# Fetching an expert's two rows with one gather, and working on them a step apart

## The chip, the cores and the metric

The kernel runs on one core of a Trainium2 chip. Its time is the device time of one execution in microseconds (us). The engines are TensorE (PE, with its weight loads PEld), VectorE (DVE), ScalarE (ACT), GpSimd (POOL) and SyncE (SP); each works through its own queue in order, and queues wait for each other by semaphores. DMAs are issued from SP, ACT and POOL; the indirect ones (gathers by a column of row numbers) from POOL.

## The reference, cut to what matters

Two transformer-like blocks over 512 tokens of 1024 features, fp32. The change is in the expert layer of the first block: each token has 8 heads x 16 chosen experts, 128 (expert, gate) pairs out of 16384 experts with a row of `expert_u` and a row of `expert_v` each.

```python
def block(args):                       # 128 tokens
    xb, ib, gb = args
    ug = expert_u[ib]
    act = jax.nn.gelu(jnp.einsum("td,tkd->tk", xb, ug)) * gb
    vg = expert_v[ib]
    return jnp.einsum("tk,tkd->td", act, vg)
```

## The kernel before

`run` (L1980) calls the stages in order: `mix`, `peer`, a tail and a gate (`ple`), `ssm`, `ffn`, `attn`, `ffn`. The kernel orders its instructions by hand: code that is called first stands first in the queues of its engines. Work beside the matmuls is kept in a list `self.bg` of (cost, function) pairs, and `run_bg` (L200) takes from it at a rate per matmul unit; `later` and `tick` (L92, L97) put a function off by some units.

In `peer` (L624) the 512 tokens are treated in two ways. Tokens 128 to 511 go through a dense sweep over all experts: for each of 128 groups of 128 experts (a unit `e` of `dense`, L1002) PE multiplies a strip of `exp_u` with the normed tokens (`lin`, tile `mm`, only for groups not worked out ahead), ACT takes the Gelu, DVE multiplies with the gates `G` (tile `ga`, L1039) and splits it into a high and a low part `A` (L117 on ACT, L112 on DVE), and PE multiplies `A` with a strip of `exp_v` into six accumulators `pv` (L1077). Strips come by SP (`wr`, L135); each is split into `wh` on ACT (L148) and `wl` on DVE (L150). 56 of the 128 units have their `exp_u` part done ahead, in the stage in which the gates are made.

The first 128 tokens do without the sweep. `first_block` (L961) has, for each of the 128 pairs, a gather of one row per token (128 tokens x 1024 floats, 512 KB; L974): first the rows of `expert_u`, whose dot with the token DVE forms (L987, accumulated into a column of `s`), and, after a Gelu over all 128 columns (L991) and a product with the gates (L992), the rows of `expert_v`, which DVE adds up with the activation as a scalar (L998). The first 32 (`EARLY`) dots run while the gates are made and use quarters of the tile `x`, whose content waits in DRAM (`xd`); it is loaded back in unit 16 of the sweep (L1069). The other 96 dots and 128 sums are steps of cost 1.2 in the sweep's list, with six slots of the tile `gx` and gathers five steps ahead:

```python
            a, b, k = (0, E, 3) if i < E else (E, 2 * P, 5)
            ...
            if i + k < b:
                fetch(i + k)
```

Between these steps the list has the items of `ssm_prep` (L1158): at first small DVE operations, then 16 parts of POOL operations (`bbs` with the tiles `bu`, `bv`, `bb`, `bd`, `cn`, L1320 to L1331; `wc`, `w2`, `tn`, L1339 to L1395), a few small matmuls (`m1p`, `m2p`, L1367, L1358), copies from PSUM (`m1o`, `m2o`) and stores from ACT's queue (L1361, L1383, L1401, L1402). Behind the sweep `peer_tail` (L745) turns the sums and adds them to `x` (L761).

Of the kernel before, what the change touches and what calls it, by code (L numbers as in the profile page):

```python
# [8 lines left out]
F32 = mybir.dt.float32  # L9
F32R = mybir.dt.float32r  # L10
BF16 = mybir.dt.bfloat16
I32 = mybir.dt.int32
U16 = mybir.dt.uint16
AF = mybir.ActivationFunctionType
ALU = mybir.AluOpType
# [4 lines left out]
P = 128  # L20
# [16 lines left out]
class K:  # L37
# [586 lines left out]
    def peer(self):  # L624
        nc, I = self.nc, self.I
# [3 lines left out]
        gd = self.dp.tile([NC, P, P, TC], F32, name="gd")  # L629
        sd = self.dp.tile([R, P, TD], F32, name="sd")  # L630
        xd = self.dp.tile([P, KT, T], F32, name="xd")
        so = self.tc.tile_pool(name="po", bufs=1)
        self.first = so.__enter__().tile([P, 4, P], F32, name="first")
        st = self.tc.tile_pool(name="pk", bufs=1)
        self.st = self.pk = st.__enter__()
        iota = self.loc((P, P), tag="iota")
        nc.scalar.dma_start(iota, I["c_iota"])

        iotaP = self.bank("mmc", (P, P), "held")
# [14 lines left out]
        n = self.ap.tile([P, KT, 2, TD], F32R, tag="xn", name="n", bufs=2)  # L654
        nt = self.accs.rearrange("p a b -> p (a b)")
# [55 lines left out]
        for what, i in self.q_order()[2:]:  # L711
# [5 lines left out]
            if (what, i) == ("q", 11):  # L717
                self.run_bg(1000)
                part = self.plan_choice(vals, idx, iotaP, st_["rc"])
# [4 lines left out]
        sg = self.tc.tile_pool(name="pg", bufs=1)  # L724
        self.st = sg.__enter__()

        if self.EARLY:
            nc.scalar.dma_start(xd, self.x)
        step = self.first_block(nt)
        self.plan_gates(part, iota, iotaP, gd, step)  # L730
        self.bg_rate, self.credit = sum(c for c, _ in self.bg) / (R - done - self.RB), 0
        for e in range(done, R):
            self.lin(nr, p_s(e), w=TD)
# [143 lines left out]
    def plan_gates(self, part, iota, iotaP, gd, step):  # L877
# [80 lines left out]
        bg += [(0.0, lambda: mid(n - 1)), (0.0, lambda: back(n - 2)), (0.0, lambda: back(n - 1)), (0.0, rest)]  # L958
        self.bg += bg

    def first_block(self, nt):  # L961

        nc, I = self.nc, self.I
        gate, ei, s, act = (self.first[:, j, :] for j in range(4))
        ei = ei.bitcast(I32)
        rows = [I["rows_u"], I["exp_v"].rearrange("a b d -> (a b) d")]
        x = self.x.rearrange("p (a b) t -> p a (b t)", b=2)
        E = self.EARLY

        def slot(i):  # L970
            return x[:, i % 4, :] if i < E else self.gx[:, i % 6, :]

        def fetch(i):
            nc.gpsimd.indirect_dma_start(  # L974
                out=slot(i), out_offset=None, in_=rows[i // P], in_offset=bass.IndirectOffsetOnAxis(ap=ei[:, i % P : i % P + 1], axis=0)
            )

        def step(i):
            a, b, k = (0, E, 3) if i < E else (E, 2 * P, 5)
            if i == a:  # L980
                for j in range(a, a + k):
                    fetch(j)
            if i + k < b:
                fetch(i + k)
            g, j = slot(i), i % P
            if i < P:
                nc.vector.scalar_tensor_tensor(  # L987
                    out=g, in0=g, scalar=1.0, in1=nt, op0=ALU.mult, op1=ALU.mult, accum_out=s[:, j : j + 1]
                )
                if j == P - 1:  # L990
                    nc.scalar.activation(act, s, AF.Gelu_apprx_tanh)  # L991
                    nc.vector.tensor_tensor(act, act, gate, ALU.mult)  # L992
                return
            acc = self.gx[:, 7, :]
            if j == 0:
                nc.vector.tensor_scalar(out=acc, in0=g, scalar1=act[:, j : j + 1], scalar2=None, op0=ALU.mult)
            else:
                nc.vector.scalar_tensor_tensor(out=acc, in0=g, scalar=act[:, j : j + 1], in1=acc, op0=ALU.mult, op1=ALU.add)  # L998

        return step  # L1000

    def dense(self, nr, gd, sd, xd, step):  # L1002

        nc = self.nc
        TC, R, TD, GG = self.TC, self.R, self.TD, self.GG
        NC = TD // TC
        A, G, S = {}, {}, {}
        pv = [self.px_(name="pv") for _ in range(4)]
        pv += [self.bank(tag, name="pv") for tag in ("mmb", "mmc")]
        self.mm_tags, self.few = ("mma",), True  # L1010
        gx = self.gx = self.ap.tile([P, 8, 8 * P], F32, tag="xn", name="gx", bufs=2)
        items = [(1.2, lambda i=i: step(i)) for i in range(self.EARLY, 2 * P)]
        prep = self.ssm_prep()
        np_ = len(prep)
        self.bg = []
        for i, it in enumerate(items):
            self.bg += prep[np_ * i // len(items) : np_ * (i + 1) // len(items)] + [it]
        total = sum(c for c, _ in self.bg)
        slow = self.SLOW
        L = self.LEAD  # L1020
        ahead = {e: i for i, e in enumerate(self.ahead())}
        rates = [1.0 if e + L in ahead or e + L >= P else slow for e in range(P)]
        scale = total / sum(rates[:-2])
        rates = [r * scale for r in rates]

        def load(e):
            if e >= P:
                return
            if e % GG == 0:
                t = self.loc((P, NC, GG, TC), tag="G", bufs=2)  # L1030
                nc.sync.dma_start(t, gd[:, :, e : e + GG, :].rearrange("c p e t -> p c e t"))
                G[e // GG] = t
            if e in ahead:
                S[e] = self.tmp((P, TD), tag="gs")
                nc.sync.dma_start(S[e], sd[ahead[e]])

        def gated(e, s):
            t = self.tmp((P, TD), tag="ga")
            nc.vector.tensor_tensor(  # L1039
                t.rearrange("p (c t) -> p c t", t=TC), s.rearrange("p (c t) -> p c t", t=TC), G[e // GG][:, :, e % GG, :], ALU.mult  # L1040
            )
            a = self.loc((P, 2, TD), F32R, tag="A", bufs=self.LEAD + 1)
            self.split(a[:, 0, :], a[:, 1, :], t, lag=int(e > 1))
            A[e] = a

        def p_s(e):
            def f(ps):
                s = self.tmp((P, TD), tag="gs")
                nc.scalar.activation(s, ps, AF.Gelu_apprx_tanh)
                gated(e, s)  # L1050
            return f

        def unit_u(e):
            load(e + 4)
            if e in ahead:
                self.prep_to(self.at + 1 + self.LA)
                gated(e, S.pop(e))
            elif e < P:
                self.lin(nr, p_s(e), w=TD)

        self.bg_rate = 0
        for e in range(4):
            load(e)
        for e in range(L):
            unit_u(e)
        for e in range(P):
            unit_u(e + L)
            if e == 16 and self.EARLY:
                nc.scalar.dma_start(self.x, xd)  # L1069
            s, a = self.next_strip(), A.pop(e)  # L1070
            for b in range(3):
                o = slice(b * P, b * P + P)
                for i, (x, ws) in enumerate(((0, (s.hi, s.lo)), (1, (s.hi,)))):
                    for w in ws:
                        for h in range(2):
                            last = e == P - 1 and x == 1
                            nc.tensor.matmul(pv[2 * b + h], a[:, x, o], w[:, h * T : h * T + T], start=(e == 0 and i == 0 and w is s.hi), stop=last)  # L1077
            self.tick()
            self.run_bg(rates[e])
            if e == P - 2:  # L1080
                self.ple_fetch(0)
        self.run_bg(100000)
        self.drain()
        for b in range(3):
            nc.scalar.copy(gx[:, b, 0:T], pv[2 * b])
            nc.vector.tensor_copy(gx[:, b, T:], pv[2 * b + 1])
        self.mm_tags, self.few = self.ALL, False
        return gx
# [992 lines left out]
def host(inputs):  # L2081
    import numpy as np

    i = {k: np.asarray(v) for k, v in inputs.items()}
    A = {"vecs": pack_vecs(i), "c_ident": np.eye(P, dtype=np.float32)}
# [4 lines left out]
    A["w_q"] = strips(i["w_q"][0])  # L2090
    A["skT"] = np.ascontiguousarray(i["sub_keys"][0].reshape(16, P, P).transpose(2, 0, 1))
    A["exp_u"] = np.ascontiguousarray(i["expert_u"][0].reshape(P, P, KT, P).transpose(0, 3, 2, 1).reshape(P, P, KT * P))
    A["rows_u"] = np.ascontiguousarray(i["expert_u"][0])
    A["exp_v"] = np.ascontiguousarray(i["expert_v"][0].reshape(P, P, KT * P))
    for j, (p, pe, pg) in enumerate([(i["p"][0], i["w_pe"][0], i["w_pg"][0])] + [(i["p_2"][l], i["ple_w_proj_2"][l], i["ple_w_gate_2"][l]) for l in (0, 1)]):
        A[f"pT{j}"] = fm(p[0])
# [46 lines left out]
```

## Time and profile before

| | us |
|---|---|
| median of the runs (lowest, highest) | 3119.45 (3111.47, 3125.9) |
| profiled execution | 3122.41 |
| its span, first to last instruction | 3120.6 |
| PE busy in the span | 2923.9 |
| DVE busy | 2216.9 |
| ACT busy | 1266.7 |
| POOL busy | 1183.6 |

The page's span holds all stages; the change is in those of 390 to 1720 us, and most of it in the sweep, 760 to 1690 us. A share over the whole span says little of that stretch, so the views below are cut to it. A matmul's record is longer than the time until the next one starts, since matmuls are pipelined. In a group's row the last part is the engine's idle time just before such instructions, and which instruction or DMA ended it.

### The profile page before, as it was taken

What the parts mean: (1) busy time and instruction counts of PE and PEld (TensorE: products, weight loads), DVE (VectorE), ACT (ScalarE), POOL (GpSimd) and SP (SyncE); (2) the same over time, 40 slices, a digit from 0 to 9 for tenths busy, and PEclk for the clock granted to TensorE, in tenths of its full rate; (3) what the DMA queues carried; (4) which work ended last, traced back from release to release, by engine and by line L of the source; (5) the groups of instructions that cost most, each with busy time, mean ns of one, the idle gap of its engine ahead of it and who ended that gap; (6) DMA issues with size and microseconds to landing.
All of it is one profiled execution on the core that took longest, in us unless ns stands there. A gap on an engine that the chain in (4) does not pass through costs nothing. (4 is left out here: it accounts for less than half of the span.)

```text
span 3120.6 us, 39487 instructions
## 1 busy us (share of the span) xinstructions
PE 2923.9 (94%) x14359; PEld 2456.2 (79%) x14359; DVE 2216.9 (71%) x3786; ACT 1266.7 (41%) x2016; POOL 1183.6 (38%) x1032
## 2 busy tenths in 40 slices
PE   8999988888999999999998989999999998999998
PEld 6677888787888787878877768888877766888886
DVE  7946888995898878787887684565675457566665
ACT  4333256566433333333334533433344345433333
POOL 3224565653248879788886330000011011100001
PEclk9889999999999999999999989999999989999999
DMA  4124344778788888888986283233332211233322
GB/s 138 48 84 150 105 142 163 248 252 305 252 290 304 291 314 299 307 286 305 317 291 221 89 256 103 86 101 98 97 97 88 81 40 49 93 97 101 95 73 96
DMA packets 248891, 534.77 MB, mean 171 GB/s; under 512 B 36671, under 2 KB 129219, under 8 KB 248314
## 3 DMA queue, kind: packets, MB, share of 16 engines
q1 hardware_dynamic: 170570, 343.69, 33.7%
q0 software_dynamic: 38656, 140.74, 13.0%
q10 hardware_dynamic: 39472, 47.84, 4.4%
q8 instruction: 113, 1.85, 0.2%
q14 instruction: 80, 0.66, 0.1%
HBM read 468.75 MB, written 63.44 MB: 171 GB/s over the span
## 5 line engine op out<-in xcount | busy, mean ns | idle before, releaser
L150 DVE TENSOR_TENSOR wl<-wr,wh 128x1024 fp32r<-128x1024 f32 (+2 forms) x453 | 548.7, 1221 | 456.4 <-ACT wh L148 447.6
L148 ACT ACTIVATE wh<-wr 128x1024 fp32r<-128x1024 f32 (+2 forms) x552 | 545.7, 997 | 505.5 <-PE mm L163 209.9
L161 PE MATMUL mm<-xn,wh 128*128 128x512 f32 x1296 | 521.4, 402 | 12.9 <-ACT xn L119 7.6
L163 PE MATMUL mm<-xn,wh 128*128 128x512 f32 x1296 | 512.4, 395 | 5.8 <-DVE xn L114 5.8
L162 PE MATMUL mm<-xn,wl 128*128 128x512 f32 x1296 | 512.8, 396 | 2.0 <-POOL wl L150 1.9
L230 POOL TENSOR_TENSOR accs<-accs,sq 128x512 f32<-128x512 f32 x56 | 86.2, 1540 | 1014.1 <-ACT sq L229 1009.2
L1077 PE MATMUL pv<-wh,A 128*128 128x512 f32 x1536 | 443.2, 402 | 22.5 <-DVE A L112 10.1
L150 POOL TENSOR_TENSOR wl<-wr,wh 128x1024 fp32r<-128x1024 f32 x99 | 241.1, 2436 | 450.4 <-ACT wh L148 439.4
L1077 PEld LDWEIGHTS pv<-wh,A 128*128 128x128 f32 x1536 | 291.8, 193 | 89.0 <-DVE A L112 17.6
L162 PE MATMUL mm<-n,wl 128*128 128x384 f32 x1024 | 348.3, 340 | 13.5 <-DVE wl L150 11.7
L161 PE MATMUL mm<-n,wh 128*128 128x384 f32 x1024 | 352.7, 344 | 0.8 <-ACT gs L703 0.8
L163 PE MATMUL mm<-n,wh 128*128 128x384 f32 x1024 | 347.8, 340 | 3.1 <-DVE n L114 3.1
L161 PEld LDWEIGHTS mm<-xn,wh 128*128 128x128 f32 x1296 | 248.6, 192 | 68.4 <-ACT xn L119 8.1
L163 PEld LDWEIGHTS mm<-xn,wh 128*128 128x128 f32 x1296 | 248.0, 191 | 61.4 <-DVE xn L114 8.6
L162 PEld LDWEIGHTS mm<-xn,wl 128*128 128x128 f32 x1296 | 248.6, 192 | 55.9 <-POOL wl L150 2.3
L1077 PE MATMUL pv<-wl,A 128*128 128x512 f32 x768 | 245.3, 401 | 26.6 <-DVE wl L150 26.6
L117 ACT ACTIVATE A<-ga 128x384 fp32r<-128x384 f32 x128 | 67.3, 525 | 424.6 <-DVE ga L1039 421.4
L998 DVE SCALAR_TENSOR_TENSOR gx<-gx,first 128x1024 f32<-128x1024 f32 x127 | 178.9, 1409 | 59.6 <-DMA gx<-in_exp_v,first 57.9
L162 PEld LDWEIGHTS mm<-n,wl 128*128 128x128 f32 x1024 | 196.0, 191 | 17.8 <-DVE wl L150 13.9
L161 PEld LDWEIGHTS mm<-n,wh 128*128 128x128 f32 x1024 | 196.0, 191 | 5.2 <-issue 1.6
L1077 PEld LDWEIGHTS pv<-wl,A 128*128 128x128 f32 x768 | 145.9, 192 | 67.4 <-DVE wl L150 35.1
L163 PEld LDWEIGHTS mm<-n,wh 128*128 128x128 f32 x1024 | 195.9, 191 | 3.5 <-DVE n L114 3.5
(409 smaller groups left out, 5356.4 us busy)
## 6 DMA issues: line engine op xcount, KB each, us to landing
wr<-in_exp_u SPq DMA_DIRECT2D x128, 512.0 KB
wr<-in_exp_v SPq DMA_DIRECT2D x128, 512.0 KB
wr<-in_w_up SPq DMA_DIRECT2D x88, 512.0 KB
gd<-gb ACTq DMA_DIRECT2D x48, 512.0 KB
G<-gd SPq DMA_DIRECT2D x32, 768.0 KB
wr<-in_w_dn SPq DMA_DIRECT2D x64, 320.0 KB
wr<-in_w_pg SPq DMA_DIRECT2D x24, 512.0 KB
sd<-gs SPq DMA_DIRECT2D x56, 192.0 KB
```

The source lines that it names most:

```text
L117: nc.scalar.activation(hi, src, AF.Copy)
L148: nc.scalar.activation(s.hi, s.raw, AF.Copy)
L150: eng.tensor_tensor(s.lo, s.raw, s.hi.bitcast(F32), ALU.subtract)
L161: t.matmul(ps, wh, xh, start=start, stop=False)
L162: t.matmul(ps, wl, xh, start=False, stop=False)
L163: t.matmul(ps, wh, xl, start=False, stop=stop)
L230: self.later(1, lambda: nc.gpsimd.tensor_tensor(acc, acc, sq, ALU.add))
L998: nc.vector.scalar_tensor_tensor(out=acc, in0=g, scalar=act[:, j : j + 1], in1=acc, op0=ALU.mult, op1=ALU.add)
L1077: nc.tensor.matmul(pv[2 * b + h], a[:, x, o], w[:, h * T : h * T + T], start=(e == 0 and i == 0 and w is s.hi), stop=last)
```

## The change

The host lays `expert_u` and `expert_v` side by side (`rows_uv`, a row of 2048 floats per expert). For the first 32 pairs the early dots fetch the first half of a row and the sweep the second, by the row numbers 2e and 2e + 1 in a new tile `two`. For the other 96 pairs one gather fetches both halves (1 MB). There are five slots of two rows: two in `x`, three in `gx`. A step `j` of the sweep adds pair `j - 2`, fetches pair `j + 3`, takes Gelu and gate of pair `j - 1` on ACT (two activations of one column each), and forms the dot of pair `j`. Steps with a dot cost 2.4 in the list. Since `x` now holds slots, it is loaded back in unit 125, and the rates are such that the list is done by then.

```diff
-        rows = [I["rows_u"], I["exp_v"].rearrange("a b d -> (a b) d")]
+        rows = I["rows_uv"]
+        half = rows.rearrange("e (h d) -> (e h) d", h=2)
+        pairs = self.x.rearrange("p (a b) t -> p a (b t)", b=4)
+        E, k = self.EARLY, self.SLOTS - 2
...
+        def early(i):
+            if i == 0:
+                nc.vector.tensor_scalar(out=self.two[:, 0, 0:E], in0=ei[:, 0:E], scalar1=1, scalar2=None, op0=ALU.logical_shift_left)
+                nc.vector.tensor_scalar(out=self.two[:, 1, 0:E], in0=self.two[:, 0, 0:E], scalar1=1, scalar2=None, op0=ALU.bitwise_or)
...
+        def slot(j):
+            j %= self.SLOTS
+            return pairs[:, j, :] if j < 2 else self.gx[:, 2 * j - 4 : 2 * j - 2, :].rearrange("p a b -> p (a b)")
+        def fetch(j):
+            if j < E:
+                gather(slot(j)[:, 8 * P :], half, self.two[:, 1, j : j + 1])
+            else:
+                gather(slot(j), rows, ei[:, j : j + 1])
+        def gated(a, b):
+            nc.scalar.activation(act[:, a:b], s[:, a:b], AF.Gelu_apprx_tanh)
...
+        def step(j):
+            if j == 0:
+                for i in range(k):
+                    fetch(i)
+                if E:
+                    gated(0, E)
+                    nc.vector.tensor_tensor(act[:, 0:E], act[:, 0:E], gate[:, 0:E], ALU.mult)
+            if j > 1:
+                add(j - 2)
+            if j + k < P:
+                fetch(j + k)
+            if E < j <= P:
+                gated(j - 1, j)
+                nc.scalar.activation(act[:, j - 1 : j], act[:, j - 1 : j], AF.Copy, scale=gate[:, j - 1 : j])
+            if E <= j < P:
+                dot(j, slot(j)[:, 0 : 8 * P])
...
-        items = [(1.2, lambda i=i: step(i)) for i in range(self.EARLY, 2 * P)]
+        items = [(1.2 if j < E or j >= P else 2.4, lambda j=j: step(j)) for j in range(P + 2)]
...
-        scale = total / sum(rates[:-2])
+        scale = total / sum(rates[:-4])
...
-            if e == 16 and self.EARLY:
-                nc.scalar.dma_start(self.x, xd)
...
+            if e == P - 3:
+                self.run_bg(100000)
+                nc.scalar.dma_start(self.x, xd)
```

Line numbers of the changed kernel are those of its own file: the dot is L980, the gather L977, the Gelu L1004, the sum L1011, the scaled copy L1027, the product `ga` L1076, `bbs` L1358 to L1369.

POOL's queue in the middle of the sweep, around one `bbs` (`bu` to `cn`), before:

```order
L974 DMA gx<-in_exp_v,first 128x1024 x3
L1320 TENSOR_TENSOR bu_10686<-bc_10376,s_1119_6471 128x32
L1321 TENSOR_TENSOR bv_10687<-bc_10376,s_1119_6471 128x32
L1322 TENSOR_TENSOR bb_10685<-bu_10686,bv_10687 128x32
L1323 TENSOR_TENSOR bu_10686<-bc_10376,s_1119_6471 128x32
L1324 TENSOR_TENSOR bv_10687<-bc_10376,s_1119_6471 128x32
L1325 TENSOR_TENSOR bb_10685<-bu_10686,bv_10687 128x32
L1327 MEMSET bd_10694 128x128
L1328 COPY bd_10694<-bb_10685 64x4x16
L1329 COPY bd_10694<-bb_10685 64x4x16
L1331 TENSOR_SCALAR cn_10698<-bc_10376 128x64
L974 DMA gx<-in_exp_v,first 128x1024 x5
```

And with the change, around a corresponding one:

```order
L977 DMA x<-in_rows_uv,first 128x2048
L1358 TENSOR_TENSOR bu_10179<-bc_9931,s_1119_6474 128x32
L1359 TENSOR_TENSOR bv_10180<-bc_9931,s_1119_6474 128x32
L1360 TENSOR_TENSOR bb_10178<-bu_10179,bv_10180 128x32
L1361 TENSOR_TENSOR bu_10179<-bc_9931,s_1119_6474 128x32
L1362 TENSOR_TENSOR bv_10180<-bc_9931,s_1119_6474 128x32
L1363 TENSOR_TENSOR bb_10178<-bu_10179,bv_10180 128x32
L1365 MEMSET bd_10187 128x128
L1366 COPY bd_10187<-bb_10178 64x4x16
L1367 COPY bd_10187<-bb_10178 64x4x16
L1369 TENSOR_SCALAR cn_10191<-bc_9931 128x64
L977 DMA gx<-in_rows_uv,first 128x2048 x3
```

Eight gathers of 1024 columns around a block have become four of 2048. The second copy into `bd` (L1329, now L1367) waits for all gathers in flight in both. From the first `bbs` to the end POOL's queue has 195 gathers before and 102 now; in the whole program 256 and 160.

DVE's queue over one unit of the sweep (two strips, their `ga`, then the steps), before:

```order
L112 TENSOR_TENSOR A_11714<-ga_11712,A_11714 128x384
L998 SCALAR_TENSOR_TENSOR gx<-gx,first 128x1024 x2
L150 TENSOR_TENSOR wl_11748<-wr_11666,wh_11747 128x1024
L150 TENSOR_TENSOR wl_11779<-wr_11716,wh_11778 128x1024
L1039 TENSOR_TENSOR ga_11804<-gs_11802,G_11385 128x384
L998 SCALAR_TENSOR_TENSOR gx<-gx,first 128x1024 x2
```

And with the change:

```order
L112 TENSOR_TENSOR A_12249<-ga_12247,A_12249 128x384
L1011 SCALAR_TENSOR_TENSOR gx<-gx,first 128x1024
L980 SCALAR_TENSOR_TENSOR x,first<-x,accs 128x1024
L150 TENSOR_TENSOR wl_12294<-wr_12191,wh_12293 128x1024
L150 TENSOR_TENSOR wl_12325<-wr_12251,wh_12324 128x1024
L1076 TENSOR_TENSOR ga_12350<-gs_12348,G_11960 128x384
L1011 SCALAR_TENSOR_TENSOR gx<-x,first,gx 128x1024
L980 SCALAR_TENSOR_TENSOR gx,first<-gx,accs 128x1024
```

Two sums per unit have become one sum and one dot, at the same place behind `ga`.

ACT's queue with the change, around the stores of one prep part (L1439, L1440; `first` holds the activations):

```order
L1004 ACTIVATE first<-first 128x1
L1027 ACTIVATE first<-first 128x1
L148 ACTIVATE wh_10655<-wr_10568 128x1024
L117 ACTIVATE A_10661<-ga_10659 128x384
L1439 DMA m3d<-wc_1777_10348 64x2x128 x2
L1439 DMA m3d<-wc_1790_10421 64x2x128 x2
L1440 DMA csd<-tn_10505 128x256
L1004 ACTIVATE first<-first 128x1
L1027 ACTIVATE first<-first 128x1
L148 ACTIVATE wh_10697<-wr_10599 128x1024
```

The rows of one column (L1004, L1027) are new, once per unit; the others stand as they did.

## Rows read from the trace of the kernel before

**Rows 1.** view by stretches, us: each engine's busy time, granted clock, DMA share, GB/s.

```profile
950.00:1690.00 740.00, 692.88 (x3303) 593.40 (x3302) 595.27 (x606) 240.75 (x340) 622.94 (x611) 0.97 0.87 300
```

**Rows 2.** groups on POOL, 950 to 1690 us: busy us, mean ns | idle before, releasers.

```profile
L974 POOL DMA_INDIRECT gx<-in_exp_v,first x128 | 169.5, 1325 | 32.3 <-issue 22.7 <-DVE A L112 2.4 <-DVE gx L998 2.2
L974 POOL DMA_INDIRECT gx<-in_rows_u,first x60 | 81.2, 1354 | 14.3 <-issue 9.6 <-DVE A L112 1.2 <-DVE gx L987 0.9
...
L1329 POOL COPY bd<-bb 64x64 f32<-64x64 f32 x15 | 10.5, 699 | 54.7 <-DMA gx<-in_exp_v,first 33.0 <-DMA gx<-in_rows_u,first 21.6
```

**Rows 3.** timeline of POOL, 1297 to 1318 us: start, us, instruction [idle before].

```profile
1299.25 1.32 POOL L974 DMA_INDIRECT gx<-in_exp_v,first  x1 [0.30 <-issue]
...
1309.55 0.23 POOL L1329 COPY bd<-bb 64x64 f32<-64x64 f32 x1 [5.79 <-DMA gx<-in_exp_v,first]
...
1310.41 1.02 POOL L974 DMA_INDIRECT gx<-in_exp_v,first  x1 [0.16 <-issue]
```

**Rows 4.** who waited for whom, 950 to 1690 us: us, times, longest.

```profile
ACT A L117 <- DVE ga L1039: 355.2, 98, 13.1
DVE gx L998 <- DMA gx<-in_exp_v,first: 56.7, 19, 6.8
DVE gx L987 <- DMA gx<-in_rows_u,first: 44.7, 18, 5.1
...
DVE wl L150 <- ACT wh L148: 28.0, 25, 6.3
...
ACT wh L148 <- DMA wr<-in_exp_v: 26.0, 9, 9.2
```

**Rows 5.** timeline of PE, 1303.8 to 1312.5 us.

```profile
1304.28 0.33 PE L161 MATMUL mm<-n,wh 128*128 128x384 f32 x1
...
1308.44 0.62 PE L1077 MATMUL pv<-wh,A 128*128 128x512 f32 x2
...
1311.65 0.62 PE L1077 MATMUL pv<-wl,A 128*128 128x512 f32 x2
```

**Rows 6.** groups on PE, 950 to 1690 us (L161 and L163 are x440 too).

```profile
L1077 PE MATMUL pv<-wh,A 128*128 128x512 f32 x1199 | 345.8, 401 | 8.7 <-DVE A L112 6.0 <-ACT wh L148 2.6
L1077 PE MATMUL pv<-wl,A 128*128 128x512 f32 x600 | 191.8, 401 | 26.6 <-DVE wl L150 26.6
...
L162 PE MATMUL mm<-n,wl 128*128 128x384 f32 x440 | 150.4, 342 | 11.9 <-DVE wl L150 11.7
...
L1367 PE MATMUL m1p<-wc,bd 128*32 128x128 f32 x120 | 15.9, 276 | 0.0
L1358 PE MATMUL m2p<-ident,w 128*128 128x128 f32 x64 | 9.6, 272 | 0.0
```

**Rows 7.** group on DVE, 950 to 1690 us: the product over 128 columns.

```profile
L992 DVE TENSOR_TENSOR first<-first 128x128 f32<-128x128 f32 x1 | 0.3, 292 | 0.4 <-ACT first L991 0.4
```

**Rows 8.** groups on ACT: the Gelu over 128 columns, and a table load.

```profile
L991 ACT ACTIVATE first<-first 128x128 f32<-128x128 f32 x1 | 0.3, 311 | 4.1 <-DVE gx L987 4.1
...
L1049 ACT ACT_TABLE_LOAD x1 | 1.3, 1283 | 0.0
```

**Rows 9.** view by stretches: the ten us of the reload of x.

```profile
873.00:883.00 10.00, 10.00 (x52) 9.05 (x51) 8.97 (x27) 3.95 (x6) 1.25 (x2) 1.00 1.02 415
```

**Rows 10.** timelines of ACT, PE and DVE at the end of the sweep.

```profile
1687.91 0.53 ACT L117 ACTIVATE A<-ga 128x384 fp32r<-128x384 f32 x1 [2.88 <-DVE ga L1039]
...
1695.52 1.18 PE L1077 MATMUL pv<-wh,A 128*128 128x512 f32 x4 [3.85 <-DVE A L112]
...
1702.73 0.68 DVE L761 TENSOR_TENSOR x<-x,pt 128x512 f32<-128x512 f32 x1
```

**Rows 11.** the page, part 3, DMA queues: packets, MB, share of 16 engines.

```profile
q1 hardware_dynamic: 170570, 343.69, 33.7%
q0 software_dynamic: 38656, 140.74, 13.0%
```

**Rows 12.** timeline of ACT, 1303 to 1313 us: behind prep's stores.

```profile
1311.56 2.00 ACT L148 ACTIVATE wh<-wr 128x1024 fp32r<-128x1024 f32 x2 [6.83 <-DMA m3d<-wc]
```

More of the change, by code (lines that the diff above doesn't have):

```diff
@@ L632, in peer @@
         so = self.tc.tile_pool(name="po", bufs=1)
-        self.first = so.__enter__().tile([P, 4, P], F32, name="first")
+        po = so.__enter__()
+        self.first = po.tile([P, 4, P], F32, name="first")
+        self.two = po.tile([P, 2, self.EARLY], I32, name="two")
         st = self.tc.tile_pool(name="pk", bufs=1)
@@ L725, in peer @@
         self.st = sg.__enter__()
[L727 to L730, printed above, removed]
+        nc.scalar.dma_start(xd, self.x)
+        early, step = self.first_block(nt)
+        self.plan_gates(part, iota, iotaP, gd, early)
         self.bg_rate, self.credit = sum(c for c, _ in self.bg) / (R - done - self.RB), 0
@@ L959, in plan_gates @@
         self.bg += bg
+    SLOTS = 5
     def first_block(self, nt):
@@ L965, in first_block @@
         ei = ei.bitcast(I32)
-        rows = [I["rows_u"], I["exp_v"].rearrange("a b d -> (a b) d")]
+        rows = I["rows_uv"]
+        half = rows.rearrange("e (h d) -> (e h) d", h=2)
         x = self.x.rearrange("p (a b) t -> p a (b t)", b=2)
[L968 to L994, printed above, removed]
+        pairs = self.x.rearrange("p (a b) t -> p a (b t)", b=4)
@@ new lines, in first_block, with gather, dot @@
+        E, k = self.EARLY, self.SLOTS - 2
+        def gather(dst, src, j):
+            nc.gpsimd.indirect_dma_start(out=dst, out_offset=None, in_=src, in_offset=bass.IndirectOffsetOnAxis(ap=j, axis=0))
+        def dot(j, u):
+            nc.vector.scalar_tensor_tensor(out=u, in0=u, scalar=1.0, in1=nt, op0=ALU.mult, op1=ALU.mult, accum_out=s[:, j : j + 1])
+        def early(i):
+            if i == 0:
+                nc.vector.tensor_scalar(out=self.two[:, 0, 0:E], in0=ei[:, 0:E], scalar1=1, scalar2=None, op0=ALU.logical_shift_left)
+                nc.vector.tensor_scalar(out=self.two[:, 1, 0:E], in0=self.two[:, 0, 0:E], scalar1=1, scalar2=None, op0=ALU.bitwise_or)
+            for j in range(3) if i == 0 else ():
+                gather(x[:, j % 4, :], half, self.two[:, 0, j : j + 1])
+            if i + 3 < E:
+                gather(x[:, (i + 3) % 4, :], half, self.two[:, 0, i + 3 : i + 4])
+            dot(i, x[:, i % 4, :])
@@ new lines, in slot, with add @@
+        def slot(j):
[8 more added lines that the diff above has]
+            nc.scalar.activation(act[:, a:b], s[:, a:b], AF.Gelu_apprx_tanh)
+        def add(j):
+            v, a, acc = slot(j)[:, 8 * P :], act[:, j : j + 1], self.gx[:, 7, :]
@@ L995, in step @@
             if j == 0:
-                nc.vector.tensor_scalar(out=acc, in0=g, scalar1=act[:, j : j + 1], scalar2=None, op0=ALU.mult)
+                nc.vector.tensor_scalar(out=acc, in0=v, scalar1=a, scalar2=None, op0=ALU.mult)
             else:
-                nc.vector.scalar_tensor_tensor(out=acc, in0=g, scalar=act[:, j : j + 1], in1=acc, op0=ALU.mult, op1=ALU.add)
-        return step
+                nc.vector.scalar_tensor_tensor(out=acc, in0=v, scalar=a, in1=acc, op0=ALU.mult, op1=ALU.add)
@@ L1002, in dense @@
+        return early, step
     def dense(self, nr, gd, sd, xd, step):
@@ L1011, in dense @@
         gx = self.gx = self.ap.tile([P, 8, 8 * P], F32, tag="xn", name="gx", bufs=2)
-        items = [(1.2, lambda i=i: step(i)) for i in range(self.EARLY, 2 * P)]
+        E = self.EARLY
+        items = [(1.2 if j < E or j >= P else 2.4, lambda j=j: step(j)) for j in range(P + 2)]
         prep = self.ssm_prep()
@@ L1015, in dense @@
         self.bg = []
-        for i, it in enumerate(items):
-            self.bg += prep[np_ * i // len(items) : np_ * (i + 1) // len(items)] + [it]
+        costs, at, to = sum(c for c, _ in items), 0.0, 0
+        for it in items:
+            at += it[0]
+            n = round(np_ * at / costs)
+            self.bg += prep[to:n] + [it]
+            to = n
         total = sum(c for c, _ in self.bg)
@@ L2092, in host @@
     A["exp_u"] = np.ascontiguousarray(i["expert_u"][0].reshape(P, P, KT, P).transpose(0, 3, 2, 1).reshape(P, P, KT * P))
-    A["rows_u"] = np.ascontiguousarray(i["expert_u"][0])
+    A["rows_uv"] = np.concatenate([i["expert_u"][0], i["expert_v"][0]], axis=1)
     A["exp_v"] = np.ascontiguousarray(i["expert_v"][0].reshape(P, P, KT * P))
```

## The prediction

> **What bounds the kernel now.** I read first the view by stretches: 760 to 1690 us is the dense sweep, with the gathers in it, and from 950 us on the operations of `ssm_prep` that run on GpSimd stand between the gathers. In these 740 us POOL is busy 622.9 and TensorE (PE) 692.9 us [rows 1]. The groups on POOL [rows 2] account for the rest of its time: 188 gathers, 250.7 us busy (169.5 + 81.2) and 46.6 us idle before them (32.3 + 14.3, mostly "issue", in which it waited for nothing shown), and 54.7 us idle before the copy `bd` of L1329. 622.9 + 46.6 + 54.7 = 724.2 of 740: POOL hardly ever waits for another engine's compute. **It is the saturated engine there.** Its timeline [rows 3] shows a block: a gather at 1299.25, then the operations of `bbs`, in which the copy waits 5.79 us for the gathers in flight to land; only at 1310.41 do gathers go on.
>
> Who pays stands in the waits [rows 4]: VectorE (DVE) waits 56.7 + 44.7 = 101.4 us for gathers, in 37 pieces. DVE's whole idle time is 740 - 595.3 = 144.7 us [rows 1], so gathers are 70% of it. Behind those sums in DVE's queue stand the low parts `wl` for which PE waits (26.6 and 11.7 us), and `A` (6.0 us) [rows 6].
>
> How much can PE give back? Its busy time is no floor, because matmuls overlap; the cadence is. 24 of the 384-wide follow each other from 1304.28 to 1308.44, 0.1733 us each, and 14 of the 512-wide from 1308.44 to 1311.65, 0.2293 us each [rows 5]. The stretch has 1199 + 600 wide and 3 x 440 narrow ones [rows 6]: 1799 x 0.2293 + 1320 x 0.1733 = 641 us, and 25 us of small ones (15.9 + 9.6): 666 us. **The room is 740 - 666 = 74 us.** The granted clock of 0.97 [rows 1], between the two levels of 1.2 and 2.4 GHz, says that 3% of 740 = 22 us of it is lost to stretches at the lower one; the rest is standing still.
>
> The Trainium skill ("Trainium Kernel Development and Optimization", Performance Expectations) says that matmul busy time is a bad metric and that the busy share of LDWEIGHTS is a good one. By the latter, 593.4 of 740 us, the room would be 147 us; by the former, 47 us. The cadence rows lie between the two, and I go by them.
>
> **The change part by part.**
>
> *Gathers on POOL.* The 195 gathers behind the first `bbs` become 102 (counted in the order of POOL's instructions): 93 go. One costs 250.7 / 188 = 1.33 us and 46.6 / 188 = 0.25 us of idle, 1.58 us in all [rows 2]. No row shows one of 8 KB a token. Bounds: 1.02 us, as a cheap one of 4 KB took [rows 3], and twice the mean, 2.67 us. I take 1.33, since both lists have 128 rows and the instruction is otherwise the same. POOL gets back 93 x 1.58 = 147 us; at the upper bound 147 - 102 x 1.33 = 11 us.
>
> *The copy that waits for all gathers in flight* stays, with up to four of 1 MB under way in place of five of 512 KB. Its 15 waits cost 54.7 us, 3.6 us each [rows 2]. Bounds: nothing (the gathers are spaced wider) and 110 us (each waits twice as long). I take 75 us, 20 more. POOL is left with 740 - 147 + 20 = 613 us, below PE's 666: POOL no longer sets the pace; PE does, with DVE's stalls on top.
>
> *What PE gets back.* 70% of 74 us is 52 us. A gather behind each block will still be late at times, since the lead stays about three sweep units (five steps at some 1.8 a unit before, three at one a unit now). I leave one fifth: **-42 us**. The bounds are 0 and -74.
>
> *DVE.* Dots and sums keep number and shape: 0. The product over 128 columns, 0.29 us [rows 7], shrinks to 32; two integer operations over 32 columns come before the first early dot, and by the same row cost +0.6 us at most; I take +0.4.
>
> *ScalarE (ACT).* 96 x 2 activations over one column are new; the nearest row is 0.31 us over 128 columns [rows 8]: 60 us at most, on an engine that is busy 240.8 of 740 us [rows 1]. A Gelu waits for the dot of the step before. That dot stands in DVE's queue ahead of the `ga` product for which ACT waits 355.2 us anyway [rows 4], so nothing new is waited for. The sum two steps behind needs the scaled value; ahead of it DVE has at least one `wl` whose `wh` stands later in ACT's queue. Both are hidden: 0; if that cover fails, see the slower rival. One more table load falls between Exp and Sin at the start: +1.3 us [rows 8].
>
> *The reload of `x`* moves from unit 16 to unit 125. Where it is it costs PE nothing (10.00 busy of 10 us [rows 9]). At the end it is issued behind ACT's last `A`; before, that `A` stands at 1687.91, and `x` is first added to at 1702.73 [rows 10]: 14.8 us, 11 without the stall of 3.85 us between them. 2.1 MB take 5.1 us at 415 GB/s [rows 9] and 7.0 at the stretch's 300 [rows 1]. It fits: 0, at worst +5.
>
> *The tail.* PE stands 3.85 us before the last units [rows 10], behind prep's last stores in ACT's queue. Now prep and gathers end before unit 125: -3 us.
>
> *DMA bytes* are the same. Queue q0, with the gathers, takes 13.0% for 140.74 MB, q1 33.7% for 343.69 MB of mostly shorter packets [rows 11]: 1.08 and 1.02 MB per thousandth. Longer packets gain nothing by their length: 0.
>
> **Sum.** The profiled execution took 3122.4 us (span 3120.6); the median of the runs, 3119.45, is 3 us lower, which I leave aside. 3122.4 - 42 - 3 + 0.4 + 1.3 = **3079 us**.
>
> **Rivals.**
>
> *More:* with POOL free, all 74 us go: 3122.4 - 74 - 3 + 1.7 = 3047. For it: POOL's list comes out 53 us below PE's. Against: DVE's 28.0 us of waits for `wh` [rows 4], which are not the gathers'. Chance 0.10.
>
> *POOL stays saturated,* because a row of 8 KB costs twice as much (11 us back, 20 more in the copy): 3110 to 3122. For it: the trace has gathers of one size only. Chance 0.13.
>
> *The gathers crowd out the strips.* ACT waits 26.0 us for strips of `exp_v`, in 9 pieces [rows 4]. If packets twice as long add one and a half times that, 39 us, and it passes through `wh` and `wl` to PE, the gain is gone: 3079 + 39 = 3118. Against: 10 us at 415 GB/s went by with PE fully busy [rows 9], so the engines have room. The Trainium skill ("DMA: Bandwidth & Descriptors", Queues, rings and completion order) says that an engine goes round its queues packet by packet. By that rule longer packets take a larger share from the strips; no row shows both lengths side by side. Chance 0.06.
>
> *Slower: ACT holds the sums.* The two small activations stand behind prep's stores, for which ACT's next activation waited 6.83 us [rows 12]. If DVE's sum waits for them, with some 2.5 us of `m1o` and `m2o` ahead, each of 15 parts costs DVE 9.4 us: 141 us, against the 101.4 for gathers that it saves. That is +40: 3162. It decides from 101.4 / 15 = 6.8 us a part on. Against: the `wl` ahead of the sum. Chance 0.10.
>
> *The change relieves POOL, but PE's stalls hang on ACT's stores,* and DVE's waits only move from the gather to `wh`: 40% of the gain, 3122 - 17 = 3105. Chance 0.06.
>
> **How the numbers follow.** The forecast has the rest, 0.55, and reaches from 3062 to 3098 with its terms' bounds. A measurement of this kernel can tell 0.5%, 15.6 us, from no change: below 3104 is faster. Faster: 0.55 + 0.10 + 0.05 of the cases near 3104 = 0.70. Same: 0.20. Slower: 0.10. The range runs from the larger gain to the unchanged cases, 3047 to 3122; outside lie the slower rival and a little on either side.
>
> **What would show it.** Right: POOL's busy time in the sweep falls by 100 us or more, DVE's waits for gathers fall below 40 us, the sweep from the first `bbs` on is some 40 us shorter, and its granted clock rises above 0.97. A gather of 2048 columns near 1.3 us shows the first step right, near 2.7 wrong. The forecast is wrong if DVE's sums (L1011) wait for ACT L1027, if the copy of `bd` waits over 100 us, or if the first addition to `x` waits for its reload.

## The result, and the profile after

The changed kernel takes **3078.1 us** (median; 3077.74 to 3078.62), the kernel before, run beside it, 3122.2: a ratio of 0.986, with a 95% interval of 0.9839 to 0.988. A later set of runs gave 0.9827 (0.9802 to 0.9852). The forecast was 3079. The page's busy times over the whole span:

```profile
PE 2908.9 (95%) x14359; PEld 2445.6 (79%) x14359; DVE 2218.9 (72%) x3788; ACT 1303.4 (42%) x2209; POOL 1093.8 (36%) x936
```

PE does the same matmuls; POOL has lost 90 us, ACT gained 37.

Where it was gained stands in the view by stretches, in columns as [rows 1], here from 950 to 1640 us, as far as both kernels are in the sweep; before:

```profile
950.00:1640.00 690.00, 644.49 (x3065) 551.75 (x3064) 553.86 (x569) 223.40 (x316) 580.27 (x571) 0.97 0.87 302
```

and with the change:

```profile
950.00:1640.00 690.00, 668.83 (x3248) 573.87 (x3247) 599.46 (x638) 275.23 (x529) 524.70 (x507) 0.99 0.89 321
```

In the same 690 us PE did 3248 matmuls in place of 3065, at a granted clock of 0.99 in place of 0.97, and POOL was busy 525 us in place of 580. The sweep ends earlier. The timeline around its end:

```profile
1653.40 0.62 PE L1112 MATMUL pv<-wh,A 128*128 128x512 f32 x2
...
1657.15 1.28 DVE L762 TENSOR_TENSOR x<-x,pt 128x512 f32<-128x512 f32 x2
```

The first addition to `x`, at 1702.73 us before [rows 10], begins at 1657.15, 45.6 us earlier; the span (now 3076.5) is 44.1 shorter. So all of the gain is in the sweep. The groups on POOL, 950 to 1640 us, which answer to [rows 2]:

```profile
L977 POOL DMA_INDIRECT gx<-in_rows_uv,first x55 | 78.2, 1421 | 46.2 <-DVE gx L1011 37.2 <-issue 6.6 <-DVE x L980 0.3
L977 POOL DMA_INDIRECT x<-in_rows_uv,first x38 | 52.4, 1378 | 28.9 <-DVE gx L1011 17.0 <-DVE gx L980 6.3 <-issue 4.1
...
L1367 POOL COPY bd<-bb 64x64 f32<-64x64 f32 x15 | 7.6, 504 | 40.2 <-DMA x<-in_rows_uv,first 17.7 <-DMA gx<-in_rows_uv,first 16.4 <-issue 6.0
```

A gather of 128 x 2048 costs POOL 130.6 / 93 = 1.40 us, hardly more than the 1.33 of one of 128 x 1024 [rows 2]. And POOL now waits for DVE (37.2 + 17.0 + 6.3 us), that is, for a slot to come free: the gatherer is ahead of the user. The waits of the same stretch say it from the other side:

```profile
ACT A L117 <- DVE ga L1076: 285.9, 99, 7.1
DVE wl L150 <- ACT wh L148: 87.8, 46, 7.4
...
ACT first L1004 <- DMA m3d<-wc: 47.1, 9, 7.7
```

DVE's 101.4 us of waits for gathers [rows 4] are gone: no such row is left (one of 7.4 us stands ahead of the stretch). In their place stands DVE's wait for `wh`, 87.8 us, three times what it was (28.0).

### The profile page after: what moved, and what is told of

Same layout as the page of the kernel before. It is cut to its first block, busy times and chain, and to the rows that moved or that the text cites. A ratio compares the mean times of both kernels' runs of the same rounds, so it can differ in the third digit from the quotient of the medians.

```text
span 3076.5 us, 39413 instructions
## 1 busy us (share of the span) xinstructions
PE 2908.9 (95%) x14359; PEld 2445.6 (79%) x14359; DVE 2218.9 (72%) x3788; ACT 1303.4 (42%) x2209; POOL 1093.8 (36%) x936
## 5 line engine op out<-in xcount | busy, mean ns | idle before, releaser
L161 PE MATMUL mm<-xn,wh 128*128 128x512 f32 x1296 | 520.9, 402 | 14.3 <-ACT xn L119 8.9
L163 PE MATMUL mm<-xn,wh 128*128 128x512 f32 x1296 | 512.4, 395 | 5.8 <-DVE xn L114 5.8
L161 PE MATMUL mm<-n,wh 128*128 128x384 f32 x1024 | 350.6, 342 | 0.8 <-ACT gs L705 0.8
L163 PE MATMUL mm<-n,wh 128*128 128x384 f32 x1024 | 345.9, 338 | 3.1 <-DVE n L114 3.1
L161 PEld LDWEIGHTS mm<-xn,wh 128*128 128x128 f32 x1296 | 248.5, 192 | 69.3 <-ACT xn L119 8.9
L163 PEld LDWEIGHTS mm<-xn,wh 128*128 128x128 f32 x1296 | 247.7, 191 | 61.4 <-DVE xn L114 8.3
L161 PEld LDWEIGHTS mm<-n,wh 128*128 128x128 f32 x1024 | 194.5, 190 | 4.9 <-issue 1.4
L163 PEld LDWEIGHTS mm<-n,wh 128*128 128x128 f32 x1024 | 194.0, 189 | 3.4 <-DVE n L114 3.4
L1670 ACT ACTIVATE uc<-up,vec 128x512 f32<-128x512 f32 x88 | 71.8, 816 | 203.8 <-DVE up L1668 203.8
```

Source lines behind the costliest of these rows:

```text
L161: t.matmul(ps, wh, xh, start=start, stop=False)
L163: t.matmul(ps, wh, xl, start=False, stop=stop)
L1670: nc.scalar.activation(c, u, AF.Identity, scale=w(2), bias=cb[:, m : m + 1])
```

## The experiments

Four sets of runs, each beside the kernel before on its chip (3122 to 3129 us from set to set), so ratios are compared and not microseconds. The theory is the prediction's: the number of gathers among `ssm_prep`'s operations on POOL was the price. The first rival is that it was the new order: a longer lead, both rows of an expert mixed, sums two steps behind. Windows below are 950 to 1640 us where no other is given.

| kernel | ratio to before (95%) | DVE waits for gathers, us | mean `wl` on DVE, ns |
|---|---|---|---|
| before | 1 | 95.0 | 1403 |
| changed | 0.986 (0.9839 to 0.988) | 0 | 1380 |
| e9_after, the same again | 0.9827 (0.9802 to 0.9852) | 0 | 1382 |
| e1_split | 0.9981 (0.9965 to 0.9997) | 74.5 | 1377 |
| e2_lean (of before) | 0.9777 (0.9754 to 0.98) | 0 | 1331 |
| e3_dummy | 0.9951 (0.9932 to 0.997) | 9.6 | 1480 |
| e4_tail (of before) | 1.0023 (1.0006 to 1.004) | 100.7 | 1415 |
| e5_fill | 0.9872 (0.9848 to 0.9897) | 12.6 | 1381 |
| e6_nodelay | 0.9964 (0.995 to 0.9977) | 0 | 1400 |
| e7_sp | 0.9794 (0.9774 to 0.9814) | 0.3 | 1348 |
| e8_leanfill (of before) | 0.9852 (0.9831 to 0.9873) | 56.7 | 1332 |
| e10_before_sp | 0.9967 (0.9951 to 0.9984) | 122.6 | 1426 |
| e11_sp_all | 0.9851 (0.9831 to 0.9872) | 0 | 1342 |
| e12_fill2 | 1.0061 (1.004 to 1.0083) | 115.9 | 1375 |

**e9_after: the yardstick of the last set.**

> The changed kernel once more, beside the others of this set, as what they are measured against: 0.984 to 0.988 of the kernel before.

3078.5 us, 0.9827, just below the expected range; DVE's waits and operations as in the table. The same kernel thus gave 0.986 and 0.9827 in two sets: differences of 0.3% between sets are not told apart.

**e1_split: the count of gathers alone, undone.**

```diff
-                gather(slot(j), rows, ei[:, j : j + 1])
+                gather(slot(j)[:, 0 : 8 * P], half, both[:, j : j + 1])
+                gather(slot(j)[:, 8 * P :], half, both[:, P + j : P + j + 1])
```

(`both` holds 2e and 2e + 1, written once into the free eighth of `gx`.)

> The changed kernel, but each of the 96 pairs is fetched by two gathers of 1024 columns into the two halves of the same slot; order, lead, slots and sums as changed. Theory (POOL's time in the sweep is what was bought): 96 more gathers at 1.4 + 0.25 us put some 150 us back on POOL, which had about 85 us to spare; POOL waits for nothing again, DVE waits for gathers 60 us or more, and the time is 3100 to 3122. Rival (the new order, lead or mixing of the two rows is what helps): 3078 within 8.

3119.6 us: 0.9981. Of POOL's groups and the waits:

```profile
L977 POOL DMA_INDIRECT gx<-in_rows_uv,gx x110 | 140.0, 1272 | 27.8 <-issue 18.9 <-DVE wl L150 3.0 <-DVE A L112 2.4
L977 POOL DMA_INDIRECT x<-in_rows_uv,gx x73 | 98.5, 1349 | 18.0 <-issue 12.3 <-DVE wl L150 1.8 <-DVE gx L980 0.9
```

```profile
DVE gx L980 <- DMA gx<-in_rows_uv,gx: 55.4, 18, 6.7
...
DVE x L980 <- DMA x<-in_rows_uv,gx: 19.1, 8, 4.8
```

POOL waits mostly for "issue" again, DVE waits 74.5 us for gathers, and nearly the whole gain is gone. Beside a saturated POOL, order, lead, delays, the moved reload and the new spread of `ssm_prep`'s items over the list (by cost, in place of by count) are together worth no more than the 0.2% that is left. The theory holds, the rival falls. The number of transfers doubles here too; e2_lean and e12_fill2, below, change POOL's time and no transfer.

**e2_lean: the same room on POOL, made in the kernel before.**

```diff
                 G.tensor_tensor(w, a[0], b[r], ALU.mult)
-                G.tensor_tensor(x, a[1], b[1 - r], ALU.mult)
-                G.tensor_tensor(w, w, x, ALU.add if r else ALU.subtract)
...
                     G.tensor_tensor(o, h[0], l[r], ALU.mult)
-                    G.tensor_tensor(x, h[1], l[1 - r], ALU.mult)
-                    G.tensor_tensor(o, o, x, ALU.add if r else ALU.subtract)
```

> The kernel before, in which ssm_prep leaves out two of the three POOL operations that make each w2 and each tn (the tables of the state space stage are then one product only): 128 POOL operations or 155 us less in the sweep, gathers and their order untouched. Theory: the gain of the change comes back without the change, 3065 to 3092, with DVE's waits for gathers under 45 us. Rival (order, lead or the moved reload helped): 3112 to 3126.

3058.3 us, 0.9777: the gain comes without any change to the gathers, and more of it than was expected. 3126.3 - 3058.3 = 68 us is nearly all of the 74 that the cadence of PE left. Why more than the change, which freed as much of POOL? Two kernels ask.

**e3_dummy and e5_fill: a product or a memset behind each gather.** Both put 96 operations of about 0.95 us on the changed kernel's POOL; the product reads its tile (which one more memset clears ahead of the first step), the memset reads nothing.

```diff
                 gather(slot(j), rows, ei[:, j : j + 1])
+                idle = self.gx[:, 6, 0 : 2 * P]
+                nc.gpsimd.tensor_tensor(idle, idle, idle, ALU.mult)
```

```diff
                 gather(slot(j), rows, ei[:, j : j + 1])
+                nc.gpsimd.memset(self.gx[:, 6, :], 0.0)
```

> The changed kernel with one more POOL operation behind each of the 96 gathers, a product of 128x256 with itself in a free slot, that nobody waits for; about 1.3 us each, 125 us on POOL, no DMA more. Theory (POOL's time, not the number of transfers): 3092 to 3118, near the kernel with split gathers. Rival (split gathers cost by their transfers, semaphores or completion): 3078 within 8 while the split kernel is slow.

> The changed kernel with a POOL operation behind each of the 96 gathers as in e3_dummy, but one that reads nothing: a memset of 1024 columns of the free slot, estimated at 1.0 to 1.4 us from the 0.20 us that the memset of bd takes for 128 columns. In e3_dummy DVE hardly waited for gathers (27 us), and its operations were longer (wl 1480 against 1380 ns). Theory A (POOL's time is what costs): 3100 to 3120, DVE waits for gathers 40 us or more. Theory B (e3_dummy lost its time by POOL products that lengthen DVE's operations beside them): 3076 to 3092, wl near 1380 ns.

e3_dummy 0.9951, e5_fill 0.9872. The first met its theory's number, but not by its mechanism, as DVE's waits show. The operations on POOL cost the same, as e3_dummy's group, over 915 to 1700 us,

```profile
L1003 POOL TENSOR_TENSOR gx<-gx 128x256 f32<-128x256 f32 x96 | 90.4, 941 | 1.9
```

and e5_fill's, over 950 to 1640 us, show:

```profile
L1002 POOL MEMSET gx<- 128x1024 f32 x93 | 90.5, 973 | 0.1
```

In both DVE hardly waits for gathers. But the `wl` of the changed kernel, of e3_dummy and of e5_fill are, in the groups on DVE,

```profile
L150 DVE TENSOR_TENSOR wl<-wr,wh 128x1024 fp32r<-128x1024 f32 x153 | 208.1, 1380 | 87.8 <-ACT wh L148 87.8
```

```profile
L150 DVE TENSOR_TENSOR wl<-wr,wh 128x1024 fp32r<-128x1024 f32 x147 | 214.6, 1480 | 62.6 <-ACT wh L148 62.6
```

```profile
L150 DVE TENSOR_TENSOR wl<-wr,wh 128x1024 fp32r<-128x1024 f32 x148 | 201.5, 1381 | 82.8 <-ACT wh L148 77.9 <-ACT first L1028 4.8
```

Of `wl` the products lengthen the mean, the memsets don't. All five kinds (`wl`, dot, sum, `ga`, `A`) together, by their means in the groups on DVE, are 36 to 41 us longer in e3_dummy than as many of the changed kernel's, by its two traces, and 5 to 10 us in e5_fill; the kernels lost 28 to 38 and 4 to 14 us. In e5_fill itself, operations of DVE that spent over half of their time beside a memset and none beside a product have, kind by kind, the median of those with nothing on POOL beside them (`ga` 548 and 551 ns, by 19 and 8 of them; sums 1274 and 1279 ns, by 13 and 9). So theory B of e5_fill holds, with the time at the upper edge of its range: 90 us of POOL's time cost the changed kernel little, and e3_dummy's loss is in DVE's own instructions. How one is lengthened stands in e5_fill's timeline of DVE:

```profile
1004.03 0.55 DVE L1077 TENSOR_TENSOR ga<-gs,G 128x384 f32<-128x384 f32 x1
1004.50 2.65 DVE L1012 SCALAR_TENSOR_TENSOR gx<-gx,first 128x1024 f32<-128x1024 f32 x1
...
1014.36 1.27 DVE L1012 SCALAR_TENSOR_TENSOR gx<-x,first,gx 128x1024 f32<-128x1024 f32 x1
```

and of POOL:

```profile
1003.81 0.98 POOL L1002 MEMSET gx<- 128x1024 f32 x1
1004.73 0.70 POOL L1388 TENSOR_TENSOR wc<-s,bc 128x288 f32<-128x288 f32 x1
1005.37 0.69 POOL L1389 TENSOR_TENSOR wcx<-s,cn 128x288 f32<-128x288 f32 x1
1006.14 1.68 POOL L1390 TENSOR_TENSOR wc<-wc,wcx 128x288 f32<-128x288 f32 x1
...
1012.07 0.81 POOL L1390 TENSOR_TENSOR wc<-wc,wcx 128x288 f32<-128x288 f32 x1
```

`ga` beside a memset takes 0.55 us. The sum that meets two products takes 2.65 us, where the same operation with nothing beside it takes 1.27: 1.27 + 0.70 + 0.69 = 2.66, as if it stood aside for both. The product behind them meets the rest of that sum and takes 1.68 in place of 0.81. In the trace of before 25 `A` of 384 columns that ran wholly beside gathers took 0.547 us, and 15 beside products 0.878. So gathers and memsets leave DVE alone, and products and DVE's operations hold each other up. The Trainium skill ("SBUF — State Buffer", SBUF: two separate sides) says that DVE and GpSimd share a pair of ports as an exclusive lock for a whole instruction, and that a DVE operation with two SBUF inputs meets it only against a GpSimd operation that reads SBUF; in that these rows agree. Which of two goes first the rows leave open: the sum's record starts at 1004.50 and the first product's at 1004.73, and the product keeps its 0.70 us.

**e12_fill2: where the room on POOL ends.** e5_fill with a second memset behind each gather.

> The changed kernel with two memsets of 1024 columns behind each gather, 186 us of POOL time that reads nothing. From 950 to 1640 us the changed kernel's POOL is busy 525 of 690 us and waits some 55 us on what it can't pass (copies of bd, issue): 110 us to spare. The 90 us of e5_fill fitted and cost little. Theory (POOL's time costs nothing until the room is used, then a microsecond each): 75 us over, about 0.986 + 0.024 = 1.010, range 1.003 to 1.02. Rival (it costs in proportion, twice e5_fill): 0.988 to 0.998.

3146.4 us, 1.0061, which is 68 us above the changed kernel of the same set. POOL hardly waits for a slot any more (2 us before its gathers, in place of 61), and DVE waits for gathers again:

```profile
DVE gx L980 <- DMA gx<-in_rows_uv,first: 76.9, 24, 8.1
...
DVE x L980 <- DMA x<-in_rows_uv,first: 39.0, 12, 9.6
```

With 110 us to spare, 90 us cost 4 to 14 (0.9872 against 0.983 to 0.986) and 186 us cost 68, near the 75 by which they pass the room. In these two runs a microsecond of POOL costs little up to there, and about its full length behind it.

**e8_leanfill: room or reads, in the kernel before.** As e2_lean, with a memset of 1024 columns for each operation left out.

```diff
                 G.tensor_tensor(w, a[0], b[r], ALU.mult)
-                G.tensor_tensor(x, a[1], b[1 - r], ALU.mult)
-                G.tensor_tensor(w, w, x, ALU.add if r else ALU.subtract)
+                G.memset(self.gx[:, 6, :], 0.0)
+                G.memset(self.gx[:, 6, :], 0.0)
```

> The kernel before with the same 128 POOL operations of w2 and tn left out as in e2_lean, and a memset of 1024 columns of a free slot in the place of each (the tables are one product only). POOL's time stays near that of before, but it reads 155 us less. Theory A (POOL's time is what costs): 3105 to 3126. Theory B (e2_lean gained because DVE's operations got shorter): 3060 to 3090, with wl near 1330 ns.

0.9852, by its number theory B. But a memset took 0.95 us in place of the 1.2 of an operation left out, so POOL also got 155 - 128 x 0.95 = 33 us back, and DVE still waits 56.7 us for gathers; it isn't a clean split. If those 33 us count in full, as the microseconds beyond the room did in e12_fill2, 3129.1 - 3084.5 - 33 = some 12 us are left for the shorter operations on DVE (`wl` 1332 against 1403 ns). By the means of the five kinds, DVE's operations are 31 us shorter here than as many of the kernel before, and 29 us in e2_lean; what part of that the kernel's time gets back, no run separates. How much of e2_lean is the one and how much the other stays open to that extent.

**e6_nodelay: the two delays, undone.**

```diff
-            if j > 1:
-                add(j - 2)
             if j + k < P:
                 fetch(j + k)
-            if E < j <= P:
-                gated(j - 1, j)
...
             if E <= j < P:
                 dot(j, slot(j)[:, 0 : 8 * P])
+                gated(j, j + 1)
...
+            if j < P:
+                add(j)
```

> The changed kernel without its delays: in step j the dot of pair j, its Gelu and gate on ACT, and its sum on DVE follow each other at once; fetches, slots and lead stay. Theory: DVE waits in each of 96 steps for a round trip through ACT's queue, 1 to 3 us behind wh and the stores, 100 to 290 us, of which the 85 us that DVE idles can hide a part: 3100 to 3230. Rival (the delays buy nothing, ACT is idle enough): 3078 within 8.

3116.1 us, 0.9964, near the lower end. In the waits:

```profile
DVE gx L1011 <- ACT first L1026: 106.5, 89, 10.5
ACT first L1004 <- DVE gx L980: 67.4, 45, 3.0
```

89 times DVE stands before a sum, 1.2 us on the mean, though no gather is late. Without the delays most of what the wider gathers buy is given back: the wait for the row is exchanged for a wait for its activation.

**e4_tail: the list's end alone, in the kernel before.**

```diff
-        scale = total / sum(rates[:-2])
+        scale = total / sum(rates[:-4])
...
+            if e == P - 3:
+                self.run_bg(100000)
```

> The kernel before, with only the list's end moved: rates over all but the last four units, and what is left of the list is worked off in unit 125. Theory: the tail is worth 3 us, 3114 to 3122, no difference that the rounds can tell from the kernel before. Rival (a good part of the gain is that the list ends earlier): 3085 to 3108.

1.0023: no gain, a loss of 0.06 to 0.4%; the rival falls, and the 3 us of the theory don't show. DVE waits for gathers as before (105.6 us from 950 to 1690, against 101.4 in [rows 4]). A guess that no run tests: while POOL is saturated, a list that must end two units earlier presses harder.

**e7_sp, e10_before_sp, e11_sp_all: whose is the new wait?** The changed kernel's wait for `wh` might come from the stores in ACT's queue. One part's block, on ACT's timeline of the changed kernel:

```profile
1319.55 3.85 ACTq L1439 DMA_DIRECT2D m3d<-wc  x4
1323.50 0.55 ACTq L1440 DMA_DIRECT2D csd<-tn  x1
1324.09 0.59 ACTq L1350 DMA_DIRECT2D bc<-in_ssm_bc  x1
1324.73 0.20 ACT L1004 ACTIVATE first<-first 128x1 f32<-128x1 f32 x1 [4.71 <-DMA m3d<-wc]
...
1325.16 1.99 ACT L148 ACTIVATE wh<-wr 128x1024 fp32r<-128x1024 f32 x2
```

Six issues of 0.55 to 0.62 us each, with 1.3 us between the first two of them, hold ACT 4.7 us, and two `wh` stand behind them. e7_sp gives the stores of `m3d` and `csd` to SP; e10_before_sp does so in the kernel before; e11_sp_all moves the load of `bc` and the stores of `m1o` and `m2o` too.

```diff
-                        nc.scalar.dma_start(self.m3d[64 * r : 64 * r + 64, ps_, g, :], src)
-                nc.scalar.dma_start(self.csd[:, ps_], d["t"])
+                        nc.sync.dma_start(self.m3d[64 * r : 64 * r + 64, ps_, g, :], src)
+                nc.sync.dma_start(self.csd[:, ps_], d["t"])
```

> The changed kernel with the stores of m3d and csd issued from SP's queue in place of ACT's; five issues a part, 0.6 us each, that now stand before ACT's next wh (a block of 4.7 us a part in the trace). Theory (what is left of DVE's waits is for wh, 97 us, and comes from ACT's store blocks): 3055 to 3073, DVE's waits for wh under 70 us. Rival (the waits for wh come from the order A, activations, wh in every unit): 3074 to 3082. A third case: SP stands at a store behind POOL and strips come late: 3085 or more.

> The kernel before with the stores of m3d and csd issued from SP as in e7_sp. Theory (with POOL saturated, ACT's blocks are not what ends last): within 0.6% of the kernel before, 0.994 to 1.002. Rival (ACT's stores are a cost of their own in either kernel, and the 20 us of e7_sp come here too): 0.990 to 0.994.

> e7_sp with the rest of ssm_prep's DMAs on SP too: the load of bc and the stores of m2o and m1o, four issues a part of 0.4 to 0.6 us. Theory (ACT's issues are the rest of DVE's waits for wh, 74 us in e7_sp): 0 to 10 us below e7_sp, ratio to before 0.976 to 0.980. Rival (SP stands behind ACT's copies of m1o and m2o, and strips come late): above e7_sp, 0.981 to 0.990.

e7_sp takes 3062.6 us, 0.9794: faster than the kernel before, and by the medians 0.3 to 0.7% under the changed one; but its interval overlaps that of e9_after (0.9802 to 0.9852), so the smaller figure isn't clear of noise. DVE's waits for `wh` fell to 74.1 us (under 70 was expected) and `wl` to 1348 ns, and PE reached

```profile
950.00:1640.00 690.00, 678.48 (x3324) 589.25 (x3322) 604.21 (x648) 284.47 (x539) 516.37 (x508) 0.99 0.91 328
```

76 matmuls more than the changed kernel, 16 of which stand behind the sweep, which ends sooner. In the kernel before the same edit gives 0.9967, as its theory has it, while POOL sets the pace: DVE's waits for `wh` fall from 26.9 to 8.2 us there, and those for gathers rise from 95.0 to 122.6. That its 10 us are less than what e7_sp gains is not shown: the two gains overlap. e11_sp_all goes too far, 0.9851, in the range of its rival. ACT's and SP's waits in it:

```profile
ACT wh L148 <- DMA wr<-in_exp_u: 73.5, 21, 7.6
ACT wh L148 <- DMA wr<-in_exp_v: 71.9, 26, 7.3
```

```profile
SPq L1421 <- ACT first L1004: 94.1, 13, 10.3
...
SPq L1399 <- ACT first L1004: 75.4, 14, 9.8
```

SP stands 94.1 + 75.4 us at the stores of `m1o` and `m2o`, whose sources ACT has yet to write (the rows name L1004, which stands right behind the copies in ACT's queue: one copy of `m1o` ends at 986.43, and its store is issued at 986.45), the strips behind them come late, and ACT waits 145 us for strips. In e7_sp SP waits 4.4 us in all for POOL: the data of the stores that went well was mostly ready when SP came to them.

## Why the prediction was right

*POOL saturated, gathers the price:* shown. e1_split gives the gain back by the number of gathers alone, e2_lean makes it with the gathers untouched, e12_fill2 takes it away with the gathers untouched: the room on POOL ends between its two memsets and e5_fill's one.

*A gather of 2048 columns at 1.33 us:* 1.40. The upper bound of 2.67, and with it the rival by which POOL stays saturated, falls.

*POOL's busy time down by 100 us or more:* not quite. Over the whole span it fell from 1183.6 to 1093.8, by 90 us. From 915 us to the sweep's end the gathers gave 119 us (142 in place of 260, by the groups), but `ssm_prep`'s own operations went from 402 to 423 us. A likely reason is that they meet DVE's work more often: of its operations of the five kinds, 43% stood beside a product for over half of their time before, and 52% do now (950 to 1640 us).

*The copy of `bd` at +20 us:* wrong in sign. It waited 54.7 us [rows 2] and now 40.2, also for 15 copies. Why was not tried.

*-42 us in the sweep:* with the tail's 3 it was 45, and 45.6 was measured at the sweep's end. That it came so near is in part luck. The 70% is the gathers' share of DVE's idle time, and no run shows that PE's room divides by it. The room itself holds: e2_lean got 68 of the 74 us, so that the rival by which all of it goes fell for this change, but the sum of the cadence did not. That part of the room was left on the table is right, but the step named the wrong holder: gathers are no longer late behind a block (no row); what is left is the wait for `wh`, 87.8 us, and DVE's lengthened operations. e7_sp gets some 10 to 20 us of that back, by the medians; what holds `wh` in its other 74 us no run tells. "Where a stall goes, what is late next" was asked only of the sums, not of `wh`.

*DVE 0:* by number and shape, yes. By duration the step missed what POOL does to it. Taking the excess of each `wl`, dot, sum, `ga` and `A` over the median of its kind with no product beside it (950 to 1630 us) gives 82 us before and 101 with the change, for 6 to 11% more of these operations. Their greater number accounts for some 7 of the 19 us; the other 12 or so are a term that stood in neither column. The gathers that went never lengthened DVE; the products that stayed do, and meet it more often.

*ACT's small activations 0, the sum two steps behind hidden:* shown. Sums wait 0.1 us in all for ACT in the changed kernel; without the delays it is 106.5 us, 1.2 us a step, not the 9.4 us a part of the slower rival.

*The reload of `x` 0:* right. On the timelines of ACT and DVE the `A` ahead of it starts at 1644.57 and the reload is issued at 1644.71; the page has 8.5 us to its landing (7.0 was taken), so about 1653.2, and the first addition begins at 1657.15. The room was 12.6 us in place of 11, the reload was longer by about as much, and 4 us are left, as worked out.

*The tail at -3:* open. The stall of 3.85 us [rows 10] is gone, but e4_tail shows that an earlier end of the list is no gain by itself. The sum would have been 3082 without it, and came out as well.

*The small terms:* the two integer operations took 0.21 and 0.18 us on DVE, and the extra table load is there (43 in the program, 42 before); what they cost the whole, no run separates.

*Gathers crowd out the strips:* no. ACT's `wh` waited 26.0 us for `exp_v` [rows 4] and 3.3 for `exp_u`, and now 9.7 and 13.3, from 915 to 1660 us, with 4.1 more for `exp_v` before a small activation: 29 us before and 27 now.

*PE's stalls hang on ACT's stores:* perhaps in part, but behind the gain and not in place of it: e7_sp adds 10 to 20 us to a gain of 44, by the medians, with intervals that overlap at the lower figure.

*The forecast's own bounds,* 3062 to 3098, don't follow from the terms: with 0 and -74 in the sweep alone the sum runs from 3047 to 3121. The measured 3078.1 lies inside either.

## What to carry to other kernels

An indirect gather is paid by POOL per instruction, hardly by the width of the rows (each here has 128 row numbers; no run varied that): rows that are always used together belong side by side in DRAM. It pays as far as POOL is saturated and no further, and only if the consumer's next wait (here the activation) is moved out of the way too. Before giving POOL arithmetic, look at what DVE does beside it, and move a DMA issue to another queue only if its data is ready when the queue gets there.

## What the runs showed of the hardware

- A product on POOL and an operation of DVE on two SBUF inputs hold each other up, in the rows above by whole instructions: a sum took 1.27 alone and 2.65 beside two products, a product 0.81 and 1.68; `A` took 0.55 us alone and 0.88 beside products. Gathers (0.547 us for `A`) and memsets (0.55 for `ga`) don't lengthen DVE's.
- A gather on POOL, on the mean: 1.27 to 1.35 us for 128 x 1024 in e1_split, 1.38 to 1.42 for 128 x 2048.
- Issuing one of these stores or loads from ACT holds ACT's queue 0.55 to 0.62 us for the most part; six in a row, with 1.3 us between two of them, were 4.7 us in which no activation ran.
